# Modulation row blocks loaded through the ring of raw weight tiles: one ring of four in place of three plus one

## The chip, the cores and the metric

One core of a Trainium2 chip runs the whole program; nothing is split over cores. The metric is the device time of one execution in microseconds (us). In the profile PE is TensorE's matmul side and PEld its weight loads, DVE is VectorE, ACT is ScalarE, POOL is GpSimd and SP is SyncE, which here only issues DMAs.

## The reference, cut to what matters

One inference step of a two-layer backbone over 640 tokens (128 of a context prompt, 512 of a sample). Each layer is a feed-forward block (FFN), a mixer, and a second FFN; the norms, the gates and the residual adds are modulated by nine vectors per layer that come from a conditioning vector through a large matrix `w_mod`:

```
sc = jax.nn.silu(cond)
for i in range(DEPTH):                                   # 2 layers, cond = c_ctx for the prompt, c for the sample
    m = (sc @ w_mod[i] + b_mod[i]).reshape(cond.shape[0], N_MOD, D_MODEL)
    hn = modulate(rms_norm(x, norm_g[i, 0]), m[:, 0], m[:, 1])
    x = x + 0.5 * m[:, 2][:, None] * swiglu(hn, ffn_w_gate[i, 0], ffn_w_up[i, 0], ffn_w_down[i, 0])
    hn = modulate(rms_norm(x, norm_g[i, 1]), m[:, 3], m[:, 4])
    x = x + m[:, 5][:, None] * mixer_i(hn)                # SSD + pooling in layer 0, gMLP + convolution in layer 1
    hn = modulate(rms_norm(x, norm_g[i, 2]), m[:, 6], m[:, 7])
    x = x + 0.5 * m[:, 8][:, None] * swiglu(hn, ffn_w_gate[i, 1], ffn_w_up[i, 1], ffn_w_down[i, 1])
```

All arrays are fp32; D_MODEL is 1024, the FFN's inner width is 2816, and `w_mod` holds 2 x 1024 x 9216 numbers.

## The kernel before, in words

**Weights.** Every fp32 weight block is loaded by SP into a raw tile (`raw_tile`, L206), then written as two fp32r tiles, a rounded high part by ACT (`wh`, L216) and the remainder by DVE (`wl`, L217), both in `w_split`. TensorE multiplies with these parts, three matmuls for one product. Raw tiles (`wr`) come from a ring named "raw" of RB = 3 tiles of 128x1024 fp32 at most; the split tiles come from a ring of nine (WB = 9). A raw tile is free for the next load when its last reader on DVE is done.

**The FFN.** It runs four times, called here by layer and place FFN(0,0), FFN(0,1), FFN(1,0), FFN(1,1). The 22 column blocks of its inner width are worked off in four groups (of 6, 5, 5 and 6 blocks). In a group the column blocks come first (`products`, matmuls on L745): seven block products each, whose weights (`wgu`) come as raw tiles of 128x1024 (L206) and 128x512 (L206) and as a tile `ws` of sums, loaded by L228, L229 and an accumulating DMA of POOL (L230). Then follows the down-projection of the group (`out_phase`, `out_add`, matmuls on L382 to L384): eight blocks `m`, each with one raw tile `in_wd` of 128x768 or 128x640, whose result is added to the residual by an accumulating DMA of POOL (L441). The DVE instruction on L763 stands near the end of each of the 19 column blocks that are worked off this way in one FFN; the text uses its starts as marks.

**The modulation.** Only the first two of the 18 vectors come from TensorE. The other 16 take 128 "items" on DVE: an item is a row block `wm` of 128x1024 fp32 (512 KB), loaded by SP on L306, and two reductions over its columns on DVE (L313, one for each conditioning vector, 128x1024 each), with a small operation on L318 or L321 behind some. `mod_item` does an item and at its end calls `mod_load` for the next. `pump` lets a fixed number of items go after each column block (`rate_j`) and after each down-projection block (`rate_m`), so that in an FFN most items fall into the down-projections. The tile `wm` has one buffer: the next row block is loaded when both reductions of the last one are done.

**Order.** TensorE's order is the order in which the code is written. On the other engines a list scheduler places the instructions by priority (the order of the code) and by when it believes that buffers are free; on the chip each engine then runs its own list in that order, and an instruction that waits holds up all behind it. This holds for SP's list of DMAs too.

Of the kernel before, what the change touches and what calls it, by code (L numbers as in the profile page):

```python
# [10 lines left out]
F32 = mybir.dt.float32  # L11
# [5 lines left out]
P = 128  # L17
D = 1024
# [9 lines left out]
NH = 16  # L28
EPS = 1e-6
WB = 9  # L30
RB = 3
NSTD = 3
TAP_EARLY = 400
PE_TAPS = 16
# [37 lines left out]
def build(tc, ap):  # L72
# [3 lines left out]
    with ctx:  # L76
        ctx.enter_context(tc.manual_schedule(engines={mybir.EngineType.PE}))
        cpool = ctx.enter_context(tc.tile_pool(name="consts", bufs=1))
        wpool = ctx.enter_context(tc.tile_pool(name="weights", bufs=1))
# [8 lines left out]
        def nm(p):  # L88
            uid[0] += 1
            return f"{p}_{uid[0]}"  # L90
# [113 lines left out]
        def raw_tile(src, n, m):  # L204
            raw = wpool.tile([P, n, m], F32, tag="raw", name=nm("wr"), bufs=RB)
            nc.sync.dma_start(out=raw, in_=src.rearrange("p (n m) -> p n m", m=m))  # L206
            return raw
# [71 lines left out]
        def open_mod():  # L279
            crow[:] = [state["pool"].tile([P, D], F32, tag=f"crow{i}", name=nm("crow"), bufs=1) for i in range(2)]  # L280
            junk[:] = [state["pool"].tile([P, D], mybir.dt.bfloat16, tag="junk", name=nm("junk"), bufs=1)]
            for i, t in enumerate(crow):
                nc.scalar.dma_start(out=t, in_=ap["cc"][i].partition_broadcast(P))
                S.activation(out=t, in_=t, func=AF.Silu)
            mod_load()
# [15 lines left out]
        def mod_load():  # L301
            it = next(items, None) if not ahead else None
            if it is not None:
                L, idx, c = it
                w = wpool.tile([P, D], F32, tag="wm", name=nm("wm"), bufs=1)
                nc.sync.dma_start(out=w, in_=ap["wm"][L, idx * KC + c])  # L306
                ahead.append((it, w))

        def mod_item():
            (L, idx, c), w = ahead.pop()  # L310
            with tc.issue_after(state["paced"]):
                for cond in range(2):
                    V.tensor_tensor_reduce(out=junk[0], in0=w, in1=crow[cond], scale=1.0,  # L313
                                           scalar=cvc("b_mod", L * 72 + idx * KC + c), op0=ALU.mult, op1=ALU.add,
                                           accum_out=mod[:, L, idx, c, cond:cond + 1])
                m = mod[:, L, idx, c, :]
                if idx in (1, 4, 7):
                    V.tensor_scalar(out=m, in0=m, scalar1=1.0, scalar2=cvc("norm_g", (L * 3 + idx // 3) * 8 + c),  # L318
                                    op0=ALU.add, op1=ALU.mult)
                elif idx in (2, 8):  # L320
                    V.tensor_scalar(out=m, in0=m, scalar1=0.5, scalar2=None, op0=ALU.mult)  # L321
            done.add((L, idx, c))
            mod_load()
# [1238 lines left out]
```

## Time and profile before

| | |
|---|---|
| median of 3 runs | 2730.87 us (2728.39 to 2733.53) |
| the profiled execution | 2715.63 us, of which the span from first to last instruction is 2713.9 us |
| busy: PE, DVE, ACT, POOL | 2547.6, 1933.5, 1243.7, 154.4 us |
| mean granted TensorE clock | 0.98 |
| from HBM | 329.17 MB, 123 GB/s over the span |

The table is read with the stages in mind: PE is busy 94% of the span, but DVE, 71% busy on average, is not spread evenly, and the FFNs with many items load it more than the rest. The profiled execution was 15.2 us faster than the median.

### The profile page before, as it was taken

To read this page: it belongs to the slowest core of one execution; us is meant where nothing else is said; L and a number is where in the kernel's file an instruction comes from. 1 tells how busy PE (TensorE), PEld (TensorE's weight loads), DVE (VectorE), ACT (ScalarE), POOL (GpSimd) and SP (SyncE) were. 2 spreads that over 40 slices of the span, in tenths; PEclk is the share of its full clock that TensorE was granted. 3 is DMA by queue.
4 is the path that set the end of the run, shared out by engine and by line. 5 is a ranking of instruction groups with operands and counts; after the bars stand their busy time and mean duration, and the time that the engine had idled before them with its cause. 6 is when DMAs were issued, how large, how long until landed. Compare 5 with 4: busy or idle time off the path is not lost.

```text
span 2713.9 us, 43717 instructions
## 1 busy us (share of the span) xinstructions
PE 2547.6 (94%) x17229; PEld 2450.2 (90%) x17229; DVE 1933.5 (71%) x3265; ACT 1243.7 (46%) x2316; POOL 154.4 (6%) x255
## 2 busy tenths in 40 slices
PE   7898997989999999999999999999999999999997
PEld 5898997989989999989999999999878999999997
DVE  6867767688996876677686758776786658554465
ACT  4434443357873544444454444443222445444452
POOL 0010110000000001101000110100000000111100
PEclk9999998999999999999999999999999999999999
DMA  7476775221112366757336776743532113656651
GB/s 283 129 196 187 194 210 164 98 73 56 53 59 82 98 174 178 200 167 206 105 102 186 188 197 187 201 121 100 153 114 79 55 66 97 182 137 154 146 133 63
DMA packets 140078, 378.09 MB, mean 139 GB/s; under 512 B 17504, under 2 KB 24160, under 8 KB 139360
## 3 DMA queue, kind: packets, MB, share of 16 engines
q1 hardware_dynamic: 111568, 296.33, 33.6%
q0 software_dynamic: 24768, 71.31, 14.8%
q10 hardware_dynamic: 3536, 7.66, 0.9%
q8 instruction: 135, 2.21, 0.3%
q14 instruction: 71, 0.58, 0.1%
HBM read 329.17 MB, written 3.67 MB: 123 GB/s over the span
## 4 chain that ended last, share of the span: by engine, by line
PE 62%; DVE 10%; DMA 9%; ACT 3%; issue 2%; DVEq 0%; ACTq 0%
PE ps L745 21%; PE ps L384 12%; PE ps L382 12%; PE ps L383 12%; DMA wm<-in_wm 5%; DVE wl L217 3%; DVE junk L313 3%; DMA wr<-in_wgu 2%; PE ps L1269 1%; PE ps L1153 1%; PE ps L1333 1%; PE ps L1335 1%; PE ps L1334 1%; DVE tmp L373 1%; PE ps L1093 0%
## 5 line engine op out<-in xcount | busy, mean ns | idle before, releaser
L217 DVE TENSOR_TENSOR wl<-wr,wh 128x1024 fp32r<-128x1024 f32 (+3 forms) x393 | 389.5, 996 | 249.4 <-PE ps L383 97.9
L216 ACT CAST wh<-wr 128x1024 fp32r<-128x1024 f32 (+3 forms) x393 | 338.8, 867 | 294.5 <-PE ps L384 109.7
L384 PE MATMUL ps<-h,wl 128*128 128x320 f32 x1408 | 438.6, 312 | 9.8 <-DVE wl L217 9.8
L313 DVE CUSTOM_DVE_ANT_0 junk<-wm,crow,cv 128x1024 bf16<-128x1024 f32 x256 | 327.7, 1280 | 165.5 <-DMA wm<-in_wm 164.4
L383 PE MATMUL ps<-h,wh 128*128 128x320 f32 x1408 | 437.9, 311 | 7.4 <-DVE h L367 7.4
L745 PE MATMUL ps<-th,wh 128*128 128x320 f32 x1216 | 388.5, 320 | 54.6 <-ACT wh L216 28.2
L382 PE MATMUL ps<-h,wh 128*128 128x320 f32 x1408 | 437.8, 311 | 0.4 <-ACT h L366 0.4
L745 PE MATMUL ps<-quad,wh 128*128 128x320 f32 x1824 | 408.1, 312 | 0.0
L745 PE MATMUL ps<-th,wl 128*128 128x320 f32 x1216 | 386.8, 318 | 19.9 <-DVE wl L217 19.9
L745 PE MATMUL ps<-tl,wh 128*128 128x320 f32 x1216 | 383.9, 316 | 0.0
L382 PE MATMUL ps<-pair,wh 128*128 128x320 f32 (+1 forms) x976 | 310.8, 318 | 8.4 <-ACT pair L375 5.8
L745 PEld LDWEIGHTS ps<-quad,wh 128*128 128x128 f32 x1824 | 309.7, 191 | 0.0
L383 PE MATMUL ps<-pair,wh 128*128 128x320 f32 (+1 forms) x976 | 305.6, 313 | 2.2 <-DVE pair L377 2.1
L384 PE MATMUL ps<-pair,wl 128*128 128x320 f32 (+1 forms) x976 | 305.2, 313 | 0.0
L745 PEld LDWEIGHTS ps<-th,wh 128*128 128x128 f32 x1216 | 235.3, 194 | 64.7 <-ACT tmp L727 33.0
L745 PE MATMUL ps<-quad,wl 128*128 128x320 f32 x912 | 285.0, 313 | 7.0 <-DVE wl L217 7.0
L384 PEld LDWEIGHTS ps<-h,wl 128*128 128x128 f32 x1408 | 265.7, 189 | 14.0 <-DVE wl L217 14.0
L383 PEld LDWEIGHTS ps<-h,wh 128*128 128x128 f32 x1408 | 265.6, 189 | 9.7 <-DVE h L367 9.2
L382 PEld LDWEIGHTS ps<-h,wh 128*128 128x128 f32 x1408 | 265.9, 189 | 0.9 <-ACT h L366 0.6
L745 PEld LDWEIGHTS ps<-th,wl 128*128 128x128 f32 x1216 | 235.6, 194 | 25.6 <-DVE wl L217 25.5
L217 DVE TENSOR_TENSOR wl<-ws,wh 128x1024 fp32r<-128x1024 f32 x152 | 185.3, 1221 | 78.0 <-ACT wh L216 41.5
L745 PEld LDWEIGHTS ps<-tl,wh 128*128 128x128 f32 x1216 | 235.7, 194 | 0.0
(262 smaller groups left out, 4400.5 us busy)
## 6 DMA issues: line engine op xcount, KB each, us to landing
wm<-in_wm SPq DMA_DIRECT2D x128, 512.0 KB, 4.0
wr<-in_wgu SPq DMA_DIRECT2D x76, 512.0 KB, 4.6
ws<-in_wgu SPq DMA_DIRECT2D x152, 256.0 KB, 3.9
ws<-in_wgu POOLq DMA_DIRECT2D x76, 512.0 KB, 6.0
x<-y POOLq DMA_DIRECT2D x96, 320.0 KB, 6.1
wr<-in_wd SPq DMA_DIRECT2D x64, 384.0 KB, 3.6
wr<-in_wd SPq DMA_DIRECT2D x64, 320.0 KB, 3.6
wr<-in_wgu SPq DMA_DIRECT2D x76, 256.0 KB, 4.1
```

The source lines that it names most:

```text
L216: S.copy(hi, src)
L217: state["paced"] = V.tensor_sub(lo, src, hi).ins
L313: V.tensor_tensor_reduce(out=junk[0], in0=w, in1=crow[cond], scale=1.0, scalar=cvc("b_mod", L * 72 + idx * KC + c), op0=ALU.mult, op1=ALU.add,
L373: V.scalar_tensor_tensor(out=t[:, a - o:b - o], in0=x[c][:, a:b], scalar=mcol(L, isc, c, cond), in1=rs[:, a - o:b - o], op0=ALU.mult, op1= ...
L382: TE.matmul(ps, lhsT=wh, rhs=xh, start=start, stop=False)
L383: TE.matmul(ps, lhsT=wh, rhs=xl, start=False, stop=False)
L384: TE.matmul(ps, lhsT=wl, rhs=xh, start=False, stop=stop)
L745: TE.matmul(ps[:, :TH], lhsT=l[k], rhs=r[:, k, :], start=(first and k == 0 and n == 0), stop=(k == 3 and n == 2), skip_group_check=True)
L1153: TE.matmul(ps5_at(yp, c, q), lhsT=c5(l)[:, c, q], rhs=c5(r)[:, c, :], start=(w == 0), stop=(w == 2 or c == 0))
L1269: TE.matmul(ps[32 * q:32 * q + 32, :q1 - q0], lhsT=dg[:, 4 * m + q, :], rhs=R[q][:, 4 * m + q0:4 * m + q1], start=(m == 0), stop=(m == PE_ ...
L1333: TE.matmul(pv[c], lhsT=xh, rhs=wh[kk], start=(k == 0), stop=False)
L1334: TE.matmul(pv[c], lhsT=xh, rhs=wl[kk], start=False, stop=False)
```

## The change

The `wm` tile is no longer a buffer of its own. It takes a place in the ring "raw", which has four tiles in place of three; the total of the memory is the same (four tiles of 128x1024 fp32). What is computed, the number of instructions and the bytes moved are the same.

```diff
@@ -28,7 +28,7 @@
 NH = 16
 EPS = 1e-6
 WB = 9
-RB = 3
+RB = 4
 NSTD = 3
@@ -302,7 +302,7 @@
             it = next(items, None) if not ahead else None
             if it is not None:
                 L, idx, c = it
-                w = wpool.tile([P, D], F32, tag="wm", name=nm("wm"), bufs=1)
+                w = wpool.tile([P, D], F32, tag="raw", name=nm("wm"), bufs=RB)
                 nc.sync.dma_start(out=w, in_=ap["wm"][L, idx * KC + c])
                 ahead.append((it, w))
```

The scheduler orders three engines anew. PE's list is the same, row for row; POOL's differs in 8 lines. SP's list in the second down-projection of FFN(0,1) stood like this before (`wr` are raw weight tiles, `wm` row blocks, `in_wd` the down-projection's weights, `in_wgu` those of the column blocks; the numbers in the names tell the tiles apart):

```order
L206 DMA wr_11301<-in_wd 128x640
L206 DMA wr_11349<-in_wd 128x640
L306 DMA wm_11252<-in_wm 128x1024
L206 DMA wr_11396<-in_wd 128x640
L206 DMA wr_11444<-in_wd 128x640
L306 DMA wm_11299<-in_wm 128x1024
L206 DMA wr_11495<-in_wgu 128x1024
L306 DMA wm_11347<-in_wm 128x1024
L206 DMA wr_11501<-in_wgu 128x512
L306 DMA wm_11394<-in_wm 128x1024
L206 DMA wr_11604<-in_wgu 128x1024
```

The same stretch of SP's list in the changed kernel:

```order
L306 DMA wm_11347<-in_wm 128x1024
L206 DMA wr_11349<-in_wd 128x640
L306 DMA wm_11394<-in_wm 128x1024
L206 DMA wr_11396<-in_wd 128x640
L306 DMA wm_11442<-in_wm 128x1024
L206 DMA wr_11444<-in_wd 128x640
L306 DMA wm_11489<-in_wm 128x1024
L206 DMA wr_11495<-in_wgu 128x1024
L206 DMA wr_11501<-in_wgu 128x512
L306 DMA wm_11557<-in_wm 128x1024
L306 DMA wm_11598<-in_wm 128x1024
L206 DMA wr_11604<-in_wgu 128x1024
```

Row blocks and raw weights now alternate: `wm_11347`, which stood behind `wr_11495`, now stands five places ahead of `wr_11444`.

DVE's list at the same place before, from the split of `wr_11349` on (L313 with `junk` is a reduction, the `mod` row behind it reads its sum out):

```order
L217 TENSOR_TENSOR wl_11352<-wr_11349,wh_11351 128x640
L313 ISA junk_9423,mod<-wm_11299,crow_9421,cv 128x1024
L313 ISA mod 128x1
L313 ISA junk_9423,mod<-wm_11299,crow_9422,cv 128x1024
L313 ISA mod 128x1
L318 TENSOR_SCALAR mod<-mod,cv 128x2
L217 TENSOR_TENSOR wl_11399<-wr_11396,wh_11398 128x640
L313 ISA junk_9423,mod<-wm_11347,crow_9421,cv 128x1024
L313 ISA mod 128x1
L313 ISA junk_9423,mod<-wm_11347,crow_9422,cv 128x1024
L313 ISA mod 128x1
L217 TENSOR_TENSOR wl_11447<-wr_11444,wh_11446 128x640
```

And in the changed kernel:

```order
L217 TENSOR_TENSOR wl_11304<-wr_11301,wh_11303 128x640
L313 ISA junk_9423,mod<-wm_11299,crow_9421,cv 128x1024
L313 ISA mod 128x1
L313 ISA junk_9423,mod<-wm_11299,crow_9422,cv 128x1024
L313 ISA mod 128x1
L318 TENSOR_SCALAR mod<-mod,cv 128x2
L217 TENSOR_TENSOR wl_11352<-wr_11349,wh_11351 128x640
L313 ISA junk_9423,mod<-wm_11347,crow_9421,cv 128x1024
L313 ISA mod 128x1
L313 ISA junk_9423,mod<-wm_11347,crow_9422,cv 128x1024
L313 ISA mod 128x1
L217 TENSOR_TENSOR wl_11399<-wr_11396,wh_11398 128x640
```

Each item stands about one block earlier: the reductions of `wm_11347`, which followed the split of `wr_11396`, now stand ahead of it. Counted over DVE's whole list, the items between the last mark (L763) of a group's column blocks and the first mark of the next group were 9, 8 and 8 in FFN(0,0) and are now 11, 11 and 10.5; in FFN(0,1) there are 8, 8 and 8 in both; in FFN(1,0) they go from 8, 8 and 8 to 8, 8.5 and 9; in FFN(1,1) from 1, 0 and 0 to the same. The items that these stretches gain are missing from the other column blocks of the same FFN.

The first read of a row block now stands farther behind the instruction that frees its place. SP's list has `wm_11442` behind `wr_11396`, and its load waits for the split of `wr_11349` on DVE; between that split and the first reduction of `wm_11442` DVE's list has two items and two splits. Before, nothing but what the scheduler put between two items stood there: between the second reduction of `wm_11299` and the first of `wm_11347` one small operation and one split.

## Rows read from the trace of the kernel before

**Rows 1.** Page: busy us of the engines, and GB/s in 40 slices.
```profile
PE 2547.6 (94%) x17229; PEld 2450.2 (90%) x17229; DVE 1933.5 (71%) x3265; ACT 1243.7 (46%) x2316; POOL 154.4 (6%) x255
...
GB/s 283 129 196 187 194 210 164 98 73 56 53 59 82 98 174 178 200 167 206 105 102 186 188 197 187 201 121 100 153 114 79 55 66 97 182 137 154 146 133 63
```

**Rows 2.** Waits, whole span: us in total, times, longest us.
```profile
DVE junk L313 <- DMA wm<-in_wm: 164.4, 72, 5.2
...
PE ps L745 <- DVE wl L217: 26.9, 23, 4.7
```

**Rows 3.** Windows, first to last mark of each FFN: us, busy (count), clock, DMA share, GB/s.
```profile
113.90:495.10 381.20, 347.03 (x2239) 340.74 (x2238) 283.63 (x450) 159.38 (x290) 33.81 (x39) 0.96 0.69 188
973.50:1327.50 354.00, 335.82 (x2235) 331.99 (x2235) 247.75 (x390) 159.43 (x290) 34.68 (x40) 0.98 0.68 180
1444.70:1802.90 358.20, 338.14 (x2238) 333.95 (x2237) 264.13 (x412) 158.86 (x290) 34.77 (x47) 0.98 0.70 189
2322.80:2653.50 330.70, 328.58 (x2235) 327.53 (x2234) 175.48 (x250) 161.87 (x290) 34.48 (x40) 1.00 0.59 146
```

**Rows 4.** Windows, the three mark-to-mark stretches around FFN(0,0)'s first three down-projections, their sum.
```profile
sum 183.80, PE 168.66 PEld 165.44 DVE 117.65 ACT 70.49 POOL 23.41; mean PE 56.22 PEld 55.15 DVE 39.22 ACT 23.50 POOL 7.80
```

**Rows 5.** The same of FFN(0,1), each stretch (PE, PEld, DVE, ACT, POOL) and the sum.
```profile
992.10:1057.40 65.30, 59.81 (x397) 59.28 (x396) 40.68 (x63) 23.43 (x47) 7.79 (x9) 0.97 0.71 192
1104.30:1165.80 61.50, 54.08 (x351) 52.62 (x351) 38.15 (x60) 22.80 (x46) 7.80 (x9) 0.95 0.74 197
1212.10:1269.00 56.90, 53.75 (x355) 52.96 (x354) 38.06 (x62) 22.43 (x46) 7.82 (x9) 0.97 0.79 212
sum 183.70, PE 167.63 PEld 164.86 DVE 116.89 ACT 68.67 POOL 23.41; mean PE 55.88 PEld 54.95 DVE 38.96 ACT 22.89 POOL 7.80
```

**Rows 6.** The same of FFN(1,0), the sum.
```profile
sum 185.50, PE 171.16 PEld 168.84 DVE 115.18 ACT 70.69 POOL 23.41; mean PE 57.05 PEld 56.28 DVE 38.39 ACT 23.56 POOL 7.80
```

**Rows 7.** The same of FFN(1,1): its second stretch, and the sum.
```profile
2445.90:2496.40 50.50, 50.50 (x347) 50.50 (x346) 18.87 (x25) 23.59 (x46) 7.82 (x9) 1.00 0.62 147
...
sum 157.90, PE 157.90 PEld 157.90 DVE 60.45 ACT 71.54 POOL 23.44; mean PE 52.63 PEld 52.63 DVE 20.15 ACT 23.85 POOL 7.81
```

**Rows 8.** DVE's timeline in FFN(0,1)'s second down-projection: start, us, operation, [idle before].
```profile
1117.75 1.28 DVE L313 CUSTOM_DVE_ANT_0 junk<-wm,crow,cv 128x1024 bf16<-128x1024 f32 x1
...
1119.22 0.82 DVE L217 TENSOR_TENSOR wl<-wr,wh 128x640 fp32r<-128x640 f32 x1
1123.10 1.28 DVE L313 CUSTOM_DVE_ANT_0 junk<-wm,crow,cv 128x1024 bf16<-128x1024 f32 x1 [3.07 <-DMA wm<-in_wm]
...
1124.43 1.28 DVE L313 CUSTOM_DVE_ANT_0 junk<-wm,crow,cv 128x1024 bf16<-128x1024 f32 x1
```

**Rows 9.** DMA issues in FFN(0,1)'s second stretch: count, KB each, median us from issue to landing.
```profile
wm<-in_wm SPq DMA_DIRECT2D x8, 512.0 KB, 4.2
...
wr<-in_wgu SPq DMA_DIRECT2D x4, 512.0 KB, 4.9
...
wr<-in_wgu SPq DMA_DIRECT2D x3, 256.0 KB, 5.3
wr<-in_wd SPq DMA_DIRECT2D x2, 320.0 KB, 3.8
```

**Rows 10.** ACT's casts by shape: busy us, mean ns, idle before.
```profile
L216 ACT CAST wh<-wr 128x1024 fp32r<-128x1024 f32 x180 | 188.0, 1047 | 137.3 <-PE ps L384 91.4 <-PE ps L1335 38.0 <-DMA wr<-in_woi 5.1
...
L216 ACT CAST wh<-wr 128x512 fp32r<-128x512 f32 x84 | 52.0, 620 | 110.1 <-DMA wr<-in_wgu 75.9 <-PE ps L745 23.7 <-PE ps L384 5.4
...
L216 ACT CAST wh<-wr 128x640 fp32r<-128x640 f32 x64 | 46.3, 727 | 16.1 <-PE ps L745 9.6 <-DMA wr<-in_wd 6.1 <-ACT wh L216 0.3
```

**Rows 11.** DVE by shape, whole span: busy us, mean ns.
```profile
L217 DVE TENSOR_TENSOR wl<-ws,wh 128x1024 fp32r<-128x1024 f32 x152 | 185.3, 1221 | 78.0 <-ACT wh L216 41.5 <-PE ps L745 31.0 <-PE ps L383 2.6
...
L242 DVE TENSOR_TENSOR ws<-wr,ws 128x512 f32<-128x512 f32 x76 | 52.1, 686 | 0.8
```

**Rows 12.** DVE's waits in FFN(1,1)'s second stretch.
```profile
DVE wl L217 <- PE ps L383: 9.3, 3, 3.6
```

## The prediction

> **What bounds the kernel now.** I read the page first. PE is busy 94% of the span [rows 1], so all that can be won is PE's idle time and the time in which its clock is low. The waits come next: DVE stands idle for row blocks of the modulation 72 times, 164.4 us in all, the largest wait of DVE; PE itself waits little for one named cause, 26.9 us for `wl` splits in the column blocks [rows 2]. Whether DVE's waits reach PE is seen by setting the four FFNs beside each other, from the first mark to the last. PE has the same work in each, but FFN(1,1) has only three items left between these marks. It takes 330.7 us, with PE busy for 328.6; the others take 381.2, 354.0 and 358.2 [rows 3]. So the items cost 50.5 + 23.3 + 27.5 = 101.3 us, and this is the ceiling of any gain from them. The reader should see that part of it is clock: the granted clock is 0.96 to 0.98 where the items are and 1.00 in FFN(1,1), so PE's own busy time is longer there too.
>
> The third view says where. I cut out the nine stretches that hold a down-projection of one of the three FFNs with items, from the last mark of a group to the first of the next. They take 183.8 [rows 4], 183.7 [rows 5] and 185.5 us [rows 6], together 553.0; the same three stretches of FFN(1,1) take 157.9 [rows 7], PE busy without a gap, so nine would be 473.7. The excess is 79.3 of the 101.3. The rest of FFN(0,0), outside the stretches, takes 381.2 - 183.8 = 197.4 against 330.7 - 157.9 = 172.8, an excess of 24.6; in the other two it is 170.3 and 172.7, none. In these stretches DVE is idle though it is late: in the second of FFN(0,1) it is busy for 38.15 of 61.5 us [rows 5]. The timeline shows with what: a split ends at 1120.04, DVE stands still for 3.07 us until the row block has landed, then does two reductions [rows 8]. In FFN(1,1) DVE waits in the same place for PE to release split weights [rows 12], which is how it looks when DVE is ahead.
>
> **The change part by part.** Instructions, bytes and PE's order are the same, so the whole effect is in waits.
>
> *Row blocks.* With one buffer the load of an item starts after the last reduction of the item before; one small operation and one split, 0.82 us [rows 8], cover a landing of 4.2 us [rows 9]. In the ring a row block's place is free earlier: the first read of `wm_11442` stands two items and two splits behind the split that frees its place. A reduction takes 1.33 us from start to start [rows 8], an item 2.66, so the cover is 2 x 2.66 + 2 x 0.82 = 7.0 us against 4.2. I count the waits for row blocks in the stretches as gone. If they stayed, nothing would change; that bound is the third rival.
>
> *Raw weights.* They pay for it. Four tiles now serve both kinds, and in the down-projections the two alternate: the load of `wr_11396` waits for the second reduction of `wm_11299`, and until its split DVE has one split and one item, 0.82 + 2.66 = 3.5 us. It needs 3.8 us to land [rows 9] and 0.73 for ACT's cast [rows 10], 4.5, so the split waits 1.0 us. The next block's load is out already and has that 1.0 us on top, so it doesn't wait: four of eight blocks wait, 4.0 us a stretch. Behind them come the two column blocks that the stretch still holds. The first raw tile of 1024 columns needs 4.9 + 1.05 = 5.95 us and has 3.5 + 1.0: 1.5 us late. Its tile of 512 columns follows about 0.5 us late. The second block's tile of 512 needs 5.3 + 0.62 = 5.9 us [rows 9, 10] and has two DVE operations of 0.69 and 1.22 [rows 11], so 4.0 us late. That makes 10 us of new waits for raw weights in each stretch. The landing times come from a stretch at 197 GB/s; the same bytes in less time will stretch them, so I take 11. The bounds: 0, if DVE is so far ahead that the loads are early anyway, as in FFN(1,1), and 20 (below).
>
> *Items that move.* FFN(0,0)'s stretches gain 2 + 3 + 2.5 = 7.5 items, 20.0 us of DVE work, taken from its other column blocks; FFN(1,0)'s gain 1.5, 4.0 us.
>
> *The sum of the stretches.* DVE's busy time becomes 117.65 + 20.0 = 137.6 in FFN(0,0), 116.9 in FFN(0,1), 115.2 + 4.0 = 119.2 in FFN(1,0) [rows 4 to 6]. With 3 x 11 of waits FFN(0,0) needs 170.6, over PE's 157.9, so DVE is still the later one there. FFN(0,1) needs 39.0 + 11 = 50.0 for a stretch, just under PE's 50.5 [rows 7], so 157.9; FFN(1,0) 39.7 + 11 = 50.7, so 158.3. Together 486.8 in place of 553.0: 66 us less.
>
> *The rest of FFN(0,0).* It loses 20.0 of its 283.6 - 117.65 = 166 us of DVE work and keeps 146; FFN(1,0) has 264.1 - 115.2 = 149 there and shows no excess. That speaks for the whole 24.6, but DVE still comes out of each stretch late here, which speaks for less. I take the middle, 12.
>
> *Nothing else.* Tiles `ws` have a ring of their own. In the mixers one row block lies in the ring unread, which leaves three tiles for raw weights, as before. After the last item FFN(1,1) has four tiles in place of three, but PE has no gap there to give back.
>
> The sum is 66 + 12 = 78 us. The profiled execution took 2715.63, 2713.9 of it span, so it would take 2638. It was 15.2 us under the median of the runs; with the same gain the median goes from 2730.87 to 2653.
>
> **The transfers.** The nine stretches move, by the three that are shown, 12.54, 12.12 and 12.06 MB (length by rate [rows 5]), 12.24 on average, so 110.2 MB, and the nine items that move in add 9 x 0.524 = 4.7. In 486.8 us that is 236 GB/s; the highest of the three stretches had 212, at a DMA share of 0.79, which scales to 268 at a share of one. The first slice of the program, plain loads only, had 283 [rows 1]. So I take the transfers as possible but slower to land, which is the 11 above. The Trainium skill, "DMA: Bandwidth & Descriptors", section "Issuing engines are not separate DMA queues", speaks against the change here: DMAs issued by SP and POOL run on the same 16 engines and interleave, so row blocks that start earlier take time from raw weights and from POOL's accumulating DMAs. The same page's "Specifications" put the HBM limit of one core at about 358 GB/s, an estimate of 114.9 MB / 358 = 321 us for the nine stretches, which would bind nothing; by the 212 of the row the sum would be 542.
>
> **The rivals.** *The transfers bind.* If 212 GB/s is all that this mix of loads and accumulates gets, the stretches take 114.9 / 0.212 = 542 us, a gain of 11, and with the 12 outside 2708. For it: the share is 0.71 to 0.79 already [rows 5]. Against: the scaled 268 and the 283. Landing times between this and my 11 give all times from 2680 to 2725.
>
> *Raw weights late: slower.* Now a raw load waits behind row blocks in SP's list and for reductions on DVE. The new waits break even when DVE's 373.7 us and nine times the wait make 553.0, at 19.9 us a stretch. Seven loads of a stretch are exposed (four, and three of the column blocks), so landing 1.4 us later than rows 9 throughout decides it. At 2 us later the wait is 24, the stretches take 590, and the time is 2768. For it: landings are medians of few loads. Against: it takes 1.4 us on 3.8 to 5.3 while the traffic rises by a fifth.
>
> *The change does nothing.* If DVE's idle time were PE's slack, removing it would only make DVE wait for PE, and the time would stay at 2731. Against: PE is busy without a gap in FFN(1,1)'s stretches and idle for 61.5 - 54.1 = 7.4 us in one of FFN(0,1)'s [rows 5, 7]. It is left only if all waits come back as waits for raw weights, at the same size.
>
> **How the numbers follow.** The forecast, stretches near PE's pace in FFN(0,1) and FFN(1,0), has 0.55, with its own range from 2630 (the ceiling, 101.3) to 2680. Late landings with part of the gain, 2680 to 2725, have 0.30. No change has 0.07, slower 0.08. A measurement of this kernel can tell about 0.2%, 5.5 us. Faster by more: 0.85; within: 0.07; slower by more: 0.08. The range, 2632 to 2708, holds the forecast and most of the second case up to the bound transfers.
>
> **What would show it.** Right: DVE's waits for row blocks fall from 164.4 to under 20; FFN(0,1) and FFN(1,0) take about 331 between the first and last mark, FFN(0,0) about 356; their clock rises to 0.99 or 1.00; DVE waits there for ACT's casts and for PE; GB/s in the stretches is near 236. Wrong: waits of ACT for `in_wd` and `in_wgu` of over 15 us a stretch (landings too late), or a rate that stays near 212 with landings of 5 us and more (transfers bind), or stretches at PE's pace in FFN(0,0) too (my waits too large).

## The result and the profile after

The changed kernel takes 2652.47 us, the median of three runs (2652.02 to 2660.62), against 2730.87 before. The ratio is 0.9722, 95% interval 0.969 to 0.9754: faster by 2.8%. The profiled execution is the one of 2652.47 us, with a span of 2650.7, so nothing has to be carried over from profile to median here.

The page of the changed kernel, with PE's busy time and the 40 slices, to be set beside [rows 1]:

```profile
PE 2525.2 (95%) x17229; PEld 2434.1 (92%) x17229; DVE 1936.4 (73%) x3265; ACT 1245.7 (47%) x2316; POOL 154.4 (6%) x255
...
GB/s 283 122 225 205 214 220 168 76 70 64 48 53 88 104 207 182 204 187 196 80 116 212 182 227 210 198 93 123 133 112 64 56 72 112 175 143 147 157 120 58
...
L313 DVE CUSTOM_DVE_ANT_0 junk<-wm,crow,cv 128x1024 bf16<-128x1024 f32 x256 | 327.6, 1280 | 3.3 <-DMA wm<-in_wm 0.7
...
wm<-in_wm SPq DMA_DIRECT2D x128, 512.0 KB, 4.4
```

DVE does the same work (1936.4 against 1933.5 us) in a shorter span. In front of the reductions it now stands idle for row blocks for 0.7 us in all, where it was 164.4 [rows 2]. A row block still takes 4.4 us to land; it only starts earlier.

What raw weights pay is seen in the waits of the whole span for them, and in that of ACT's `y` activations. Before:

```profile
DVE wl L217 <- ACT wh L216: 94.9, 74, 8.7
...
ACT wh L216 <- DMA wr<-in_wgu: 77.3, 25, 6.7
...
ACT y L440 <- DMA x<-y: 33.7, 17, 5.7
...
ACT wh L216 <- DMA wr<-in_wd: 8.8, 7, 3.2
```

And after:

```profile
DVE wl L217 <- ACT wh L216: 144.3, 118, 8.7
ACT wh L216 <- DMA wr<-in_wd: 119.2, 48, 6.1
...
ACT wh L216 <- DMA wr<-in_wgu: 58.8, 43, 5.1
...
ACT y L440 <- DMA x<-y: 50.0, 21, 4.2
```

ACT's wait for `in_wd` was 8.8 us before and is 119.2, that of DVE's splits for the casts was 94.9 and is 144.3. The wait for `in_wgu` comes more often (43 times in place of 25) but is smaller in all, 58.8 us in place of 77.3. Of ACT's longer waits only a part reaches DVE: its wait for casts grew by 49 us, and that is what counts.

The windows of the four FFNs, from the first mark to the last, against [rows 3]:

```profile
116.10:466.20 350.10, 333.76 (x2226) 330.19 (x2225) 285.23 (x451) 158.37 (x289) 33.79 (x39) 0.99 0.75 205
943.20:1283.00 339.80, 331.86 (x2238) 330.13 (x2237) 248.90 (x389) 160.31 (x289) 34.12 (x40) 0.99 0.70 188
1403.30:1736.40 333.10, 329.92 (x2239) 328.12 (x2238) 264.94 (x413) 159.37 (x289) 34.84 (x47) 1.00 0.75 203
2260.10:2590.40 330.30, 326.90 (x2222) 325.59 (x2221) 175.12 (x250) 161.63 (x290) 34.40 (x40) 1.00 0.59 147
```

FFN(0,0) falls from 381.2 to 350.1, FFN(0,1) from 354.0 to 339.8, FFN(1,0) from 358.2 to 333.1; FFN(1,1), which has hardly any items, stays. The granted clock goes from 0.96, 0.98 and 0.98 to 0.99, 0.99 and 1.00, and PE's busy time falls with it, by 25.5 us in the three (some 2 us of this only because 13 matmuls of FFN(0,0) are missing from the trace; in FFN(1,1) as many are missing, and its busy time falls by 1.7).

The nine stretches with a down-projection, three for each FFN, against [rows 4 to 6]: first those of FFN(0,0) with their sum, then the second of FFN(0,1) and the sum, then the second and third of FFN(1,0) and the sum.

```profile
136.30:194.20 57.90, 57.90 (x395) 57.75 (x395) 48.05 (x78) 23.97 (x46) 7.79 (x9) 1.00 0.84 233
242.40:301.10 58.70, 54.31 (x356) 53.56 (x355) 46.71 (x72) 24.94 (x48) 7.80 (x9) 0.97 0.89 241
348.20:406.00 57.80, 52.99 (x341) 52.23 (x340) 45.65 (x73) 24.96 (x48) 7.81 (x9) 0.94 0.84 234
sum 174.40, PE 165.19 PEld 163.53 DVE 140.41 ACT 73.87 POOL 23.39; mean PE 55.06 PEld 54.51 DVE 46.80 ACT 24.62 POOL 7.80
...
1070.60:1123.30 52.70, 52.70 (x348) 52.70 (x347) 39.76 (x61) 22.79 (x46) 7.82 (x9) 0.96 0.80 215
...
sum 161.70, PE 160.36 PEld 159.68 DVE 120.01 ACT 71.59 POOL 23.46; mean PE 53.45 PEld 53.23 DVE 40.00 ACT 23.86 POOL 7.82
...
1528.30:1578.10 49.80, 49.13 (x333) 48.64 (x332) 39.57 (x59) 23.23 (x46) 7.79 (x9) 1.00 0.90 243
1625.60:1676.60 51.00, 50.77 (x346) 50.51 (x346) 41.80 (x65) 23.40 (x46) 7.78 (x9) 1.00 0.90 244
sum 157.30, PE 156.40 PEld 155.65 DVE 122.12 ACT 71.42 POOL 23.40; mean PE 52.13 PEld 51.88 DVE 40.71 ACT 23.81 POOL 7.80
```

Together 174.4 + 161.7 + 157.3 = 493.4 us in place of 553.0. In FFN(0,1) and FFN(1,0) PE is busy almost without a gap, as in [rows 7]; in FFN(0,0) it still is not, for 174.4 - 165.2 = 9.2 us.

DVE's timeline in FFN(0,1)'s second down-projection, the place of [rows 8]:

```profile
1082.95 0.83 DVE L217 TENSOR_TENSOR wl<-wr,wh 128x640 fp32r<-128x640 f32 x1 [0.77 <-PE ps L383]
1083.70 1.28 DVE L313 CUSTOM_DVE_ANT_0 junk<-wm,crow,cv 128x1024 bf16<-128x1024 f32 x1
...
1085.02 1.28 DVE L313 CUSTOM_DVE_ANT_0 junk<-wm,crow,cv 128x1024 bf16<-128x1024 f32 x1
...
1087.35 0.83 DVE L217 TENSOR_TENSOR wl<-wr,wh 128x640 fp32r<-128x640 f32 x1 [1.04 <-ACT y L440]
...
1092.50 0.83 DVE L217 TENSOR_TENSOR wl<-wr,wh 128x640 fp32r<-128x640 f32 x1 [1.52 <-ACT wh L216]
1093.24 1.28 DVE L313 CUSTOM_DVE_ANT_0 junk<-wm,crow,cv 128x1024 bf16<-128x1024 f32 x1
```

Where DVE stood for 3.07 us before a reduction, the reductions now follow the splits with no gap. The gaps have moved in front of the splits and are shorter: 0.77, 1.04, 1.52 us, behind PE's release of split tiles or behind ACT.

**Where the 63.2 us between the two profiled executions came from** (2715.63 to 2652.47): the stretches gave 553.0 - 493.4 = 59.6, the rest of FFN(0,0) 197.4 - 175.7 = 21.7; the rest of FFN(0,1) took back 178.1 - 170.3 = 7.8 and that of FFN(1,0) 175.8 - 172.7 = 3.1. What lies outside the four windows, span less their sum, went from 1289.8 to 1297.4, 7.6 more. Those five give 62.8; FFN(1,1) has the last 0.4.

### The profile page after: what moved, and what is told of

Read it like the earlier page. It is cut to its first block, busy times and chain, and to the rows that moved or that the text cites. A ratio compares the mean times of both kernels' runs of the same rounds, so it can differ in the third digit from the quotient of the medians.

```text
span 2650.7 us, 43732 instructions
## 1 busy us (share of the span) xinstructions
PE 2525.2 (95%) x17229; PEld 2434.1 (92%) x17229; DVE 1936.4 (73%) x3265; ACT 1245.7 (47%) x2316; POOL 154.4 (6%) x255
## 3 DMA queue, kind: packets, MB, share of 16 engines
q0 software_dynamic: 24768, 71.31, 15.2%
## 5 line engine op out<-in xcount | busy, mean ns | idle before, releaser
L216 ACT CAST wh<-wr 128x1024 fp32r<-128x1024 f32 (+3 forms) x393 | 339.7, 868 | 376.8 <-DMA wr<-in_wd 119.2
L745 PE MATMUL ps<-quad,wh 128*128 128x320 f32 x1824 | 406.8, 311 | 3.8 <-ACT tmp L727 3.8
L745 PE MATMUL ps<-th,wh 128*128 128x320 f32 x1216 | 382.3, 314 | 28.4 <-ACT tmp L727 22.9
L745 PE MATMUL ps<-th,wl 128*128 128x320 f32 x1216 | 380.0, 313 | 3.6 <-DVE wl L217 3.6
L745 PE MATMUL ps<-tl,wh 128*128 128x320 f32 x1216 | 379.3, 312 | 0.0
L313 DVE CUSTOM_DVE_ANT_0 junk<-wm,crow,cv 128x1024 bf16<-128x1024 f32 x256 | 327.6, 1280 | 3.3 <-DMA wm<-in_wm 0.7
L745 PEld LDWEIGHTS ps<-quad,wh 128*128 128x128 f32 x1824 | 307.7, 189 | 4.6 <-ACT tmp L727 4.5
L745 PE MATMUL ps<-quad,wl 128*128 128x320 f32 x912 | 283.5, 311 | 4.9 <-DVE wl L217 4.9
L745 PEld LDWEIGHTS ps<-th,wh 128*128 128x128 f32 x1216 | 231.4, 190 | 35.4 <-ACT tmp L727 28.4
L745 PEld LDWEIGHTS ps<-th,wl 128*128 128x128 f32 x1216 | 231.5, 190 | 4.9 <-DVE wl L217 4.9
L745 PEld LDWEIGHTS ps<-tl,wh 128*128 128x128 f32 x1216 | 231.5, 190 | 0.0
```

The lines of the kernel that those rows point to most:

```text
L216: S.copy(hi, src)
L745: TE.matmul(ps[:, :TH], lhsT=l[k], rhs=r[:, k, :], start=(first and k == 0 and n == 0), stop=(k == 3 and n == 2), skip_group_check=True)
```

## The experiments

Theory 1, on which the prediction rests: a row block has no second place, so DVE stands idle for its landing, and PE behind DVE; a place that comes free earlier removes this, and raw weights pay a part of it back. The rivals doubt one link each: that the loss is a wait at all and not DVE's own work for the items, that it is the second buffer and not the sharing, the fourth raw tile or the traffic. Times are medians. A ratio is to the kernel before on the same chip, and as its median lies between 2730.7 and 2735.7 us from chip to chip, runs of different chips are better compared by their ratios. "FFNs" are the four windows as above, in the order of the program.

**A fixed split of the same four tiles**, two for row blocks and two for raw weights:

```diff
-RB = 3
+RB = 2
-                w = wpool.tile([P, D], F32, tag="wm", name=nm("wm"), bufs=1)
+                w = wpool.tile([P, D], F32, tag="wm", name=nm("wm"), bufs=2)
```

> Row blocks keep a ring of their own, with two buffers in place of one, and raw weights have two tiles in place of three: the same four tiles, not shared. Theory 1 (what pays is that a row block can be loaded while the one before is reduced; sharing is not needed for that): DVE's waits for row blocks stay under 25 us in all (164.4 before), the FFNs come near those of the changed kernel (350.0, 339.8, 333.1), and the time lies between 2640 and 2675. Rival A (a pool of four that serves whichever kind is short is what pays; a fixed split starves the raw weights, which had three tiles): raw weights late in the column blocks, FFN(0,1) and FFN(1,0) above 350, the time above 2700.

Measured: 2672.28 us (2663.24 to 2678.42), ratio 0.9777 (0.9738 to 0.9816). Its FFNs take 348.4, 345.7, 340.5 and 339.2. Waits, whole span:

```profile
ACT wh L216 <- DMA wr<-in_wgu: 95.1, 57, 5.3
ACT wh L216 <- DMA wr<-in_wd: 87.5, 59, 4.9
...
DVE junk L313 <- DMA wm<-in_wm: 30.8, 22, 3.8
```

A second buffer for row blocks gives most of the gain without any sharing, though 30.8 us of waits for row blocks remain, where under 25 were expected. By the medians the split is 20 us slower than the ring of four, by the ratios 15, and the two intervals overlap (0.9738 to 0.9816 here, 0.969 to 0.9754 there), so that it is slower is likely but not clear of the noise. FFN(1,1), which has hardly any row blocks to wait for, goes from 330.7 to 339.2; with three raw tiles beside two for row blocks (below) it takes 328.9, so two raw tiles are too few for it.

**The ring with three tiles**, one less in all than before: the changed kernel with

```diff
-RB = 4
+RB = 3
```

> Row blocks in the ring of raw tiles as in the changed kernel, but the ring has three tiles, one less in all. Theory 1 with its price (raw weights pay for the cover of the row blocks; the price grows when the ring is short): row blocks hardly waited for, under 20 us, but raw weights late by about 2 us a block, some 14 us of new waits in each down-projection stretch where the changed kernel was reckoned at 10, and some more in the column blocks: 2690 to 2740. Rival B (raw weights have cover to spare, and only row blocks matter): as the changed kernel, 2650 to 2665.

Measured: 2711.66 us (2705.16 to 2718.98), ratio 0.9923 (0.99 to 0.9946); FFNs 365.6, 357.7, 358.5, 329.0. Waits, whole span:

```profile
DVE wl L217 <- ACT wh L216: 310.0, 192, 8.8
ACT wh L216 <- DMA wr<-in_wgu: 171.0, 78, 6.8
...
ACT wh L216 <- DMA wr<-in_wd: 142.0, 80, 6.3
```

Here the price is seen at its full size. Row blocks don't wait, but DVE's wait for casts is 310.0 us, 215 more than before, and most of the gain is gone. Sharing pays for row blocks with raw weights, and how many tiles there are decides what is left.

**No row loads**: the reductions read two resident rows.

```diff
-                w = wpool.tile([P, D], F32, tag="wm", name=nm("wm"), bufs=1)
-                nc.sync.dma_start(out=w, in_=ap["wm"][L, idx * KC + c])
+                w = None
...
-                    V.tensor_tensor_reduce(out=junk[0], in0=w, in1=crow[cond], scale=1.0,
+                    V.tensor_tensor_reduce(out=junk[0], in0=crow[1 - cond], in1=crow[cond], scale=1.0,
```

> The kernel before without the loads of row blocks: the reductions read one conditioning row times the other, both resident, so the modulation's values are not the reference's and 64 MB less are moved. DVE's work is the same. Theory 1 (the wait for the row block is the cost, not the two reductions): FFN(0,1) and FFN(1,0) at 331 to 334 us between first and last mark, FFN(0,0) at 335 to 350 since DVE's own work still fills its stretches; the time 2625 to 2650. Rival C (DVE's work or its place in the order is the cost): FFN(0,1) and FFN(1,0) stay above 345, the time above 2690.

Measured: 2616.92 us (2614.76 to 2617.51), ratio 0.9576 (0.9544 to 0.9607). Windows of its first three FFNs:

```profile
115.30:446.60 331.30, 329.07 (x2239) 328.02 (x2238) 283.62 (x450) 161.34 (x290) 33.82 (x39) 1.00 0.59 142
924.00:1255.20 331.20, 329.03 (x2238) 327.98 (x2237) 247.90 (x390) 160.84 (x290) 33.83 (x39) 1.00 0.58 142
1372.10:1703.50 331.40, 329.12 (x2239) 328.06 (x2238) 264.22 (x413) 161.32 (x290) 34.28 (x46) 1.00 0.59 142
```

DVE is busy in FFN(0,0) for 283.62 us, as before (283.63 [rows 3]), and the window falls from 381.2 to 331.3, PE's own pace. The time is under the expected 2625 and FFN(0,0) under its 335. So the items' work on DVE costs nothing; all but 2 of the 101 us over FFN(1,1) go with the loading of row blocks: the wait for it, or its traffic. DVE's order was not held fixed here: without the loads FFN(0,0)'s three stretches hold 11, 11 and 10.5 items and FFN(1,0)'s 8, 8.5 and 9, as in the changed kernel. FFN(0,1)'s hold 8 each in all three kernels, and its window falls from 354.0 to 331.2 just the same.

**Five tiles.** The ring of temporaries (128x320 fp32) is cut from ten to seven to make room for one more tile. First the control, this cut alone:

```diff
-        tpool = ctx.enter_context(tc.tile_pool(name="temps", bufs=10))
+        tpool = ctx.enter_context(tc.tile_pool(name="temps", bufs=7))
```

> Control for the three runs beside it: the kernel before with seven temporary tiles of 128x320 in place of ten, which makes room for one more tile of 128x1024. Expected by every theory: little change, 2725 to 2745. A larger change is to be taken off the others.

Measured: 2738.5 us (2732.28 to 2754.58), ratio 1.0016 (0.9998 to 1.0034): the cut costs nothing that can be told. The three that follow use the room for one more tile, each in another way.

The fifth tile as a second row block, with three raw tiles as before (`bufs=2` for `wm`):

> With seven temporary tiles: two buffers for row blocks, three raw tiles as before, nothing shared, five tiles in all. Theory 1: row blocks are covered and raw weights keep their cover, so the new waits for raw weights of the changed kernel are absent too: 15 to 25 us faster than the changed kernel less what the control loses, 2627 to 2645; FFN(0,0) 335 to 345. Rival A (sharing pays): slower than the changed kernel, over 2660.

Measured: 2647.47 us (2646.84 to 2648.78), ratio 0.9673 (0.9659 to 0.9688); FFNs 350.9, 331.4, 338.0, 328.9. The page of this kernel, the reductions and the load:

```profile
L313 DVE CUSTOM_DVE_ANT_0 junk<-wm,crow,cv 128x1024 bf16<-128x1024 f32 x256 | 327.9, 1281 | 51.6 <-DMA wm<-in_wm 49.6
...
wm<-in_wm SPq DMA_DIRECT2D x128, 512.0 KB, 5.0
```

Theory 1 is shown with it: nothing is shared, and 91 us of the control's 2738.5 are gone. But with two buffers of their own row blocks still wait for 49.6 us, half of it in FFN(0,0), and so the time is 2 us above the expected 2645 and FFN(0,0) 6 us above 345. The Trainium skill ("Perfetto Trace Analysis", "Optimization Strategy") says of a gap that repeats for a stretch on the engine that should be saturated that it can mean that memory for the next tile is missing. The runs agree for DVE, behind which PE waits here: 59 such gaps, 151.7 us, stood in the nine stretches of before, and a second tile removes most of them.

The fifth tile as a fourth raw tile, with one row block as before (`RB = 4`):

> With seven temporary tiles: one buffer for row blocks as before, four raw tiles, nothing shared, five tiles in all. Theory 1: nothing gained, since the row blocks have no more cover: as the control, within 8 us of it, and DVE's waits for row blocks stay at 150 to 180 us. Rival D (the fourth raw tile is what pays): 2650 to 2690.

Measured: 2720.18 us (2711.9 to 2726.01), ratio 0.9936 (0.9914 to 0.9958); FFNs 376.2, 349.8, 358.1, 329.4. The expectation failed: the fourth raw tile alone gives 18 us against the control, where at most 8 were expected. The waits for row blocks stay, 172.1 us (control 189.5), and ACT's wait for `in_wgu` falls from 90.7 to 59.2. By which of the two it comes was not taken apart.

The fifth tile in one ring for both kinds (`RB = 5`, `tag="raw"`):

> With seven temporary tiles: the shared ring of the changed kernel with five tiles in place of four. Theory 1: the price that raw weights pay mostly goes, as with two row buffers beside three raw tiles: 2627 to 2645. Rival E (what is left over in the changed kernel is DVE's work and PE's own waits, not raw weights that land late): 2645 to 2660, as the changed kernel.

Measured: 2632.6 us (2626.82 to 2639.01), ratio 0.9621 (0.9598 to 0.9645), the fastest here that leaves nothing out; its interval doesn't touch that of the change (0.969 to 0.9754). Windows of its first three FFNs:

```profile
115.20:454.00 338.80, 331.39 (x2236) 329.13 (x2235) 284.19 (x451) 159.10 (x290) 33.80 (x39) 0.99 0.78 212
931.00:1262.50 331.50, 329.22 (x2238) 327.99 (x2237) 248.27 (x389) 161.67 (x290) 34.71 (x40) 1.00 0.73 193
1381.90:1716.40 334.50, 329.81 (x2239) 328.13 (x2238) 264.67 (x413) 159.75 (x290) 34.33 (x46) 1.00 0.74 202
```

FFN(0,1) is at PE's pace, FFN(0,0) 7.5 us and FFN(1,0) 3.1 us over the kernel without row loads. By the medians the ring beats a fixed split of the same memory twice, 2652 against 2672 with four tiles and 2633 against 2647 with five. The second pair ran on one chip and its intervals are apart; those of the first pair overlap.

**The fifth tile taken from the split tiles** instead, with ten temporaries: the changed kernel with

```diff
-WB = 9
-RB = 4
+WB = 8
+RB = 5
```

> The shared ring with five tiles, its memory taken from the ring of split weights (eight in place of nine) and not from the temporaries (ten, as before). Theory 1: the cover of row blocks and raw weights is as with five tiles and seven temporaries, so 2627 to 2645 if the ninth split tile isn't needed. Rival G (DVE is kept ahead of PE by the split tiles, and eight are too few): PE waits more for splits, 2645 to 2680.

Measured: 2650.22 us (2648.65 to 2654.78), ratio 0.9696 (0.9668 to 0.9724). Its FFNs, 339.5, 332.0, 331.5 and 332.3, add up to those of the five tiles above; the loss lies outside them, 17 us of it in the mixers, 484.6 and 531.4 us against 477.0 and 522.2. PE's largest wait in the first of them:

```profile
PE ps L382 <- ACT wh L216: 7.3, 8, 1.0
```

ACT's casts wait there for PE to give back a split tile, 40.1 us with eight tiles and 38.1 with nine, but only with eight does PE then wait for the casts: with nine this wait is not in PE's list at that place. So a split tile is not free to take, as the temporaries were: the time lies in the rival's range.

**The traffic alone.** Row blocks are loaded as before, but the reductions read the resident rows:

```diff
-                    V.tensor_tensor_reduce(out=junk[0], in0=w, in1=crow[cond], scale=1.0,
+                    V.tensor_tensor_reduce(out=junk[0], in0=crow[1 - cond], in1=crow[cond], scale=1.0,
```

> The kernel before with the row blocks loaded as always but not read: the reductions run on the resident conditioning rows, so the modulation's values are not the reference's. The traffic is back (64 MB more than without row loads), no DVE instruction waits for it, and the raw ring keeps its three tiles; SP may issue the loads somewhat ahead of the reductions. Theory 1 (waits, on DVE, are the whole cost, and the transfers have room): as without row loads, 2615 to 2630, each FFN at 331 to 335. Rival F (the traffic itself makes raw weights and the accumulating DMAs late): 2640 or more, FFN(0,0) over 340.

Measured: 2714.71 us (2708.99 to 2719.56), ratio 0.9926 (0.9905 to 0.9948). It lies far above what was expected, and it doesn't answer the question. SP's waits, whole span, and the window of FFN(0,0):

```profile
SPq L306 <- DMA wm<-in_wm: 441.3, 125, 21.8
```

```profile
120.60:534.10 413.50, 350.93 (x2236) 345.85 (x2235) 284.79 (x451) 155.64 (x289) 34.59 (x40) 0.93 0.81 230
```

With no reader, nothing held the loads back but the one buffer. Of the 128, 17 went out ahead of FFN(0,0), 92 in it and the last 19 right behind it, up to 602.9 us; 125 times SP itself waited for the landing of the one before, with the raw weights queued behind. (The next expectation says that all 128 fell into the first FFN, which isn't quite so.) FFN(0,0) took 413.5 us, and the next two, now without row blocks, 329.0 and 331.4.

So it was done again with each load held until an item's place in DVE's list: two buffers, seven temporaries, and

```diff
                 w = wpool.tile([P, D], F32, tag="wm", name=nm("wm"), bufs=2)
+                V.tensor_copy(w[:, 0:1], state.get("last", eps_t))
                 nc.sync.dma_start(out=w, in_=ap["wm"][L, idx * KC + c])
...
+            state["last"] = mod[:, L, idx, c, 1:2]
```

> The run with unread row blocks let SP load all 128 of them in the first FFN, so it said nothing on the traffic at its usual pace. Here each load waits for the reductions of the item before, as in the kernel before (by a copy of one column of sums into the tile), into two buffers, with seven temporary tiles; the reductions still read resident rows, so the modulation's values are not the reference's, and nothing waits for a landing but that copy two items later. Theory 1 (DVE's wait is the cost, the traffic at this pace is not): FFNs at 331 to 338 us, the time 2615 to 2632. Rival F (the traffic makes raw weights and accumulating DMAs late): FFN(0,0) over 342, the time over 2638. The run with two row buffers that are read, 2647, lies on the rival's side; if this one comes out near 2620, the 25 us between them are waits for row blocks that two buffers don't cover.

Measured: 2632.16 us (2630.76 to 2641.34), ratio 0.9627 (0.9589 to 0.9665); FFNs 342.5, 332.3, 334.1, 330.6; DVE, with its copies, still waits 10 us for row blocks. It falls between: FFN(0,1) and FFN(1,0) are near PE's pace, FFN(0,0) is 11 us over it. Of the 30 us from no row loads (2617) to two row buffers that are read (2647), about 15 come with the loads themselves, in which the 128 small copies are not told from the traffic, and about 15 with waits that two buffers don't cover. Against the kernel before, each on its own chip, no row loads gain 117 us and this run 99, with all the traffic there: so the traffic is the smaller part of what row blocks cost. The ring of five, 2632.6, stands at the same place: it has no waits for row blocks left.

**The kernel before once more**, for a second profile of it:

> The kernel before, unchanged, for a second profile: the first one was of an execution 15 us under the median. If that execution was a fortunate one in the stretches with items, this one shows the FFNs with items longer than 381.2, 354.0 and 358.2 us, and the rest the same; if the 15 us lie outside the FFNs, those three stay.

Measured: 2741.27 us, one execution. Windows of its first three FFNs:

```profile
116.60:512.40 395.80, 351.96 (x2239) 345.11 (x2239) 283.26 (x450) 159.25 (x290) 33.81 (x39) 0.94 0.68 181
990.00:1350.10 360.10, 338.12 (x2238) 334.43 (x2237) 247.81 (x389) 159.60 (x290) 34.12 (x40) 0.98 0.68 177
1467.30:1827.90 360.60, 340.11 (x2237) 335.73 (x2237) 264.75 (x412) 159.24 (x291) 34.68 (x47) 0.97 0.71 187
```

This execution, 25.6 us longer than the profile on which the prediction stands, has 23.1 us of its extra time in these three FFNs (14.6, 6.1 and 2.4), and DVE's wait for row blocks is 189.9 us where it was 164.4. So these two executions differ mostly where row blocks are waited for; FFN(1,1) is 330.7 in both.

## Why the prediction was right, and where it only seemed so

**Right, and shown.** The cause: DVE's waits for row blocks reached PE. No row loads takes them all away, with DVE's work unchanged, and the FFNs run at PE's pace; a second row buffer alone takes most of them away. (With both the scheduler also moves items into the stretches of FFN(0,0) and FFN(1,0), but none in FFN(0,1).) That the ring covers the landing: 0.7 us are left. That raw weights pay: the ring of three shows it without the fourth tile. That transfers don't bind at 212 GB/s: the second and third stretch of FFN(1,0), shown above, ran at 243 and 244 GB/s, and all nine on average at 230 (length by rate, 113.7 MB in 493.4 us), where 236 were reckoned. The row of 212 was a demand, not a limit. The 268 that was scaled up from it is borne out too, at 271, in the third stretch of FFN(0,0) with the ring of five:

```profile
345.00:394.60 49.60, 49.60 (x340) 49.44 (x339) 45.04 (x73) 22.89 (x45) 7.80 (x9) 1.00 0.98 271
```

With the weighed rule of the Trainium skill ("DMA: Bandwidth & Descriptors", "Issuing engines are not separate DMA queues", that DMAs of all issuers share the same 16 engines) the trace agrees in kind, not in the size that it would have had to have: in FFN(0,1)'s second stretch row blocks went from 4.2 us to land [rows 9] to

```profile
wm<-in_wm SPq DMA_DIRECT2D x7, 512.0 KB, 4.6
...
wr<-in_wgu SPq DMA_DIRECT2D x4, 512.0 KB, 5.6
...
wr<-in_wd SPq DMA_DIRECT2D x3, 320.0 KB, 3.5
```

and the raw tiles of 512 KB from 4.9 to 5.6, while those of `in_wd` land in 3.5 where it was 3.8. The slower rival needed 1.4 us more on all of them. In the three stretches at 241 to 244 GB/s it comes nearer to that: raw tiles of 512 KB take 5.7 to 6.1 us there (4.3, 5.5 and 5.2 before) and row blocks 4.7 to 5.1 (3.3, 4.1 and 4.3), but `in_wd` 3.4 to 4.5 (5.3, 5.5 and 3.6), not longer.

**New waits for raw weights, mis-sized.** 11 us a stretch were taken. DVE's wait for casts in the nine stretches is 71.7 us, worked out from their waits one by one, and was 25.9 before, so 45.8 are new, 5.1 a stretch, half of it. In the same way the waits for row blocks in them fell from 151.7 to 0.7. The walk through one stretch gave every late load to DVE. Where DVE has to wait for PE anyway, as at 1082.95 in the timeline above, a late load costs it less; how many hide in this way was not counted. That a wait for casts need not cost time could be seen before: in FFN(1,1)'s second stretch, of which [rows 12] shows only the wait for PE, the largest wait of DVE is one for casts, and PE is busy without a gap:

```profile
DVE wl L217 <- ACT wh L216: 11.1, 4, 4.3
```

The sign named for loads that come too late, ACT waiting over 15 us a stretch, was badly chosen: it reached 15.8 to 16.7 in four of the nine, all three of FFN(0,0) among them, where DVE waits 6.6 to 9.6 us for casts, less than the 11 that were reckoned with.

**The stretches, a smaller gain than forecast, 59.6 and not 66.** The forecast took the larger of two numbers, DVE's busy time with its waits or PE's 157.9 at full clock. FFN(1,0) came as forecast (157.3 against 158.3). FFN(0,1) and FFN(0,0) are each 3.8 us over it (161.7 and 174.4). In FFN(0,1) the second stretch has PE busy throughout at a granted clock of 0.96, so PE's own time is longer than in FFN(1,1). In FFN(0,0) DVE's idle time is 174.4 - 140.4 = 34.0, as taken (33), though only 24.5 of it is for casts; its busy time is 2.8 us more than reckoned. So of the signs named for being right one failed, FFN(0,1), which takes 339.8 and not about 331; about half of that lies in its stretches and half in its rest.

**The rest of FFN(0,0), half of the excess taken, nearly all of it came**: 21.7 of 24.6, not 12. That DVE leaves each stretch late was not felt much. Two things went away there: 7.5 items, and 11.2 us of waits for row blocks, which the prediction counted in the stretches alone. The two kernels with a second row buffer move the same items and lose the same waits (their rest takes 178.9 and 177.8), so which of the two it was is not shown.

**Nothing else, wrong by some 18 us.** The rest of FFN(0,1) and FFN(1,0) takes 10.9 us longer; one single wait of PE on L745 for ACT's `tmp` (4.9 us) is a part of it. In the kernel without row loads, at PE's pace throughout, the same two take 174.8 and 176.1, so 7.9 of the 10.9 come there too, while its stretches take 155.3 to 156.5 and not 157.9: so most of it is likely work that the marks count to the rest once DVE is on time. Outside the windows it is 7.6 us; over the kernels of this study that figure runs from 1288 to 1303 where WB is nine, so whether the change does it stays open.

**The step from profile to median failed, and cancelled this.** The terms, 78 us, were to hold between profiles, where 63.2 came: 15 too many. The number was right to half a microsecond because "with the same gain" set the sum against the median too, and the profile of before had been of an execution 15.2 us under its median, while that of after is of the median itself. Against the second profile of before the difference is 88.8. The two profiles of before differ mostly in the wait that the change removes, so the fortunate one held less to gain than the median. The mechanism and the ranking were right; that the last digits agree is chance.

**What the chances left out.** That sharing is worth more than a fixed split was not asked. With five tiles it is, by 15 us; with four the 15 to 20 us are not clear of the noise. The cover explains it in kind: with two buffers of their own row blocks still wait (30.8 and 49.6 us), in the ring they don't, and where there are hardly any, as in FFN(1,1), all tiles serve raw weights. How many items a stretch holds is not what differs: 11, 11 and 10.5 in FFN(0,0), 8 each in FFN(0,1), and 8, 8.5 and 9 in FFN(1,0), in the rings of four and five and in both splits. The finer order of DVE's and SP's lists does differ and was not held fixed, so how much is cover and how much order is open.

## What to carry to other kernels

When an engine stands idle for one kind of load with a single buffer while PE waits behind it, set a stage with that load beside one without it: the difference is the ceiling, and leaving the load out confirms it in one run. Try one ring for two kinds of load, and count the tiles: here a shared ring beat a fixed split, clearly with five tiles, but one tile fewer gave most of it back, and the tile to add has to come from a ring that has slack (temporaries, at no cost that could be told) and not from one that doesn't (split tiles, 18 us). Before setting a sum against the median, see whether the profiled execution stands at it, and whether what varies is the very wait that the change removes.

## What the hardware showed that was not expected

- The kernel before varies by about 20 us between executions (2723.59 to 2743.85 over eleven runs on one chip), the kernel without row loads by 2.8 (2614.76 to 2617.51). The two profiles of before put the difference into the FFNs that have row blocks. But the ring of five, which has no waits for row blocks left, varies by 12.2 over four runs, so they are not all that varies.
- A load with no reader is no free load. With one buffer SP waited 441.3 us for the landings of its own row blocks and held the raw weights behind them.
- ACT's `y` activations waited 50.0 us for POOL's accumulating DMAs to free their tile (33.7 before). Casts that stand behind them in ACT's list may wait along though their raw weights have landed; how much of DVE's wait comes by this way was not taken apart.
